# Splitting 36 of 48 key, query and value weights ahead of time and keeping their parts in DRAM

## The chip, the cores and the metric

The kernel runs on one core of a Trainium2 chip. The metric is the device time of one execution in microseconds (us), the median of three runs. TensorE is called PE, VectorE DVE, ScalarE ACT, GpSimd POOL and SyncE SP; PEld is PE's loading of the stationary operand. SP computes nothing here, it issues DMAs.

## The reference

Two residual blocks act on one sequence of 512 tokens with 1024 channels, all in float32. The first block has a sliding window attention layer and a pooling layer. The second has two layers of a mixer and a feed forward each:

```python
for l in range(DEPTH):                       # DEPTH = 2
    h = rmsnorm_2(x, attn_norm[l])
    proj = h @ w_in[l]                       # keys, queries and values of both kinds of heads
    sb_q, sb_k, sb_v, df_q, df_k, df_v = split(proj)
    sb_out = stick_breaking_attention(sb_q, sb_k, sb_v)        # 8 heads of 64
    df_out = differential_attention(rope(df_q), rope(df_k), df_v, lam)   # 4 pairs
    x = x + concat(sb_out, norm(df_out)) @ w_o[l]
    h = rmsnorm_2(x, mlp_norm[l])
    x = x + relu(h @ w_ff1[l])**2 @ w_ff2[l]                   # 1024 -> 4096 -> 1024
```

A stick-breaking head needs a running product over the keys of each row of scores, and so a scan.

## The kernel before

The activations lie transposed, 8 tiles of 128 channels by 512 tokens. Each product with a weight keeps float32 accuracy with three passes in a rounded format: a weight `w` is split into a high part `whi` (ACT copies it in the rounded format, L385) and a low part `wlo` (DVE subtracts, L388), the activations likewise into `xh` and `xl`, and PE adds whi·xh, whi·xl and wlo·xh in PSUM. One weight tile is 128 by 8 by 128, 512 KB; `lin` runs its 24 matmuls of 512 columns. For values, `lin_tokens` takes two such tiles (two halves) and runs 96 matmuls of 256 columns.

`weights` is the helper all of them call: it has `fetch` load the tile into `wst` (2 buffers) by a DMA on SP, then makes `whi` and `wlo` (3 buffers each). So ACT can split a weight as soon as PE has finished the weight three before it. A program names the order of PE's work: `lin` yields between its 8 steps, and the heads of the mixer (`sb_head` for stick-breaking, `df_head` for differential attention) are tasks which PE's order weaves between those steps. In a stick-breaking head each query tile goes through scores on PE, a mask on DVE (L1056), a sigmoid on ACT (L1058), 1 - w on ACT (L1061, tile `sbl`), a scan on DVE (L1064, `sbr`), a product on DVE (L1065, `sbw`), and then back to PE, which transposes it (`flip`, L358); ACT and DVE split the transposed tile into `wth` and `wtl` (L1078, L1079).

The whole program is built twice. After the first build `Plan` prices every instruction (`cost`), simulates the engines, and gives an order for PE, ACT, DVE, POOL and SP; the second build is bound to those orders. Every engine takes its instructions strictly in order, so an instruction that waits holds all behind it, and on SP a DMA that waits holds the later DMAs.

The stages on the time axis of the profile: sliding window attention until about 200 us, the pooling layer (`pool_layer`) until about 360, the first mixer until 600, the first feed forward (`ff_layer`) until 960, the second mixer until 1200, the second feed forward until the end. In a mixer 24 weight tiles are needed before the output projection: 8 of keys, 8 of queries, 8 halves of values.

Of the kernel before, what the change touches and what calls it, by code (L numbers as in the profile page):

```python
# [105 lines left out]
class Plan:  # L106
# [91 lines left out]
    def cost(self, k, i):  # L198
        def free(x):
            return math.prod(n for _, n in list(x.ap)[1:])  # L200

        def psum(x):
            return "PSUM" in str(type(x.bass_ap.tensor)).upper()

        aps = [x for x in i.outs if type(x).__name__ == "PhysicalAccessPattern"]
        src = [x for x in i.ins if type(x).__name__ == "PhysicalAccessPattern"]
        e, op = self.eng[k], str(i.opcode)
        n = max([free(x) for x in aps if x.memref] or [0])
        if op == "DMACopy":
            self.dur[k] = 1040.0 if e == "Pool" else 60.0  # L210
            self.bytes[k] = 4.0 * min(math.prod(m for _, m in x.ap) for x in aps + src)
        elif e == "PE":
            self.dur[k] = max(107.0, (n + 32) / 2.4)
        elif e == "Activation":
            one = sum(1 for x in src[1:] if free(x) == 1) + (len(aps) > 1)
            self.dur[k] = 1300.0 if not aps else n / 1.2 + (51.0 if psum(src[0]) else 93.0) + 93.0 * one
        elif e == "DVE":
            small = sum(1 for x in src[1:] if free(x) == 1) + (len(aps) > 1)
            fast = op in ("TensorCopy", "TensorScalarPtr") and len(src) - small <= 1 and not any(map(psum, src + aps))
            self.dur[k] = n / (1.92 if fast else 0.96) + 69.0 + (61.0 if small else 0.0)  # L220
            self.port[k] = fast or sum(1 for x in src if free(x) > 1 and not psum(x)) > 1
        else:
            self.dur[k] = 147.0 + 2.105 * n
            self.port[k] = op != "Memset"
# [83 lines left out]
def two_blocks_kernel(ctx: ExitStack, tc: tile.TileContext, a, out, log, orders=()):  # L308
# [13 lines left out]
    def open_pool(name, tags, side=None):  # L322
        pool = tc.alloc_tile_pool(name=name, bufs=1, side=side, reuse_waits="tile")
        log["pools"].append((name, True))
        where.update({t: pool for t in tags.split()})
        return pool
# [39 lines left out]
    def fetch(src, nk=KT, first=None):  # L366
# [5 lines left out]
            order(d, acts.pop("xdma"))  # L372
        return st

    def weights(src, nk=KT):
        with tc.high_priority():
            st = staged.pop(0) if staged else fetch(src, nk)
            hi = sb([P, KT, P], F32R, "whi", 3)
            lo = sb([P, KT, P], F32R, "wlo", 3)
            if early:  # L380
                early.pop()
                nc.vector.tensor_copy(hi[:, :nk, :], st[:, :nk, :])  # L382
                nc.vector.tensor_sub(lo[:, :nk, :], st[:, :nk, :], f32(hi[:, :nk, :]))  # L383
            else:
                c = nc.scalar.activation(hi[:, :nk, :], st[:, :nk, :], AF.Copy)  # L385
                if "x" in acts:
                    order(c, acts.pop("x"))
                low[0].tensor_sub(lo[:, :nk, :], st[:, :nk, :], f32(hi[:, :nk, :]))  # L388
        return hi, lo
# [17 lines left out]
    def lin(src, xs, tag="lin"):  # L407

        nk = len(xs)
        hi, lo = weights(src, nk)  # L410
        if spread[0]:
            spread[0] += 1
            tag = ("lin", "sc")[spread[0] % 2]
        ps = yield from take_bank(tag)
        for k in range(nk):
            if isinstance(xs[k], Val):
                if xs[k].t is None or xs[k].t > pe.clock:
                    yield xs[k]
                xh, xl = xs[k].v
            else:  # L420
                xh, xl = xs[k]
            mm(ps, hi[:, k, :], xh, k == 0, False)
            mm(ps, hi[:, k, :], xl, False, False)
            mm(ps, lo[:, k, :], xh, False, k == nk - 1)
            yield None
        return ps
# [365 lines left out]
    def add_to_x(k, ps):  # L792
        nc.vector.tensor_add(x[k], x[k], ps)  # L793
        drained(ps)
# [163 lines left out]

    def pool_layer(nrm, nxt):
        pin = a["pool_in"]  # L960
        pool = open_pool("pool", "u ws pz pe pth ptl tnh og uh ul")
        outs = [Val() for _ in range(8)]
        ps_ = [Val() for _ in range(8)]
        As = [Val() for _ in range(8)]

        def on_u(t, ps):
            w = POOL_WINDOWS[t // 2]

            def go(r):
                u = sb([P, 16 + S], F32, "u", 2)  # L970
                nc.gpsimd.memset(u[:, 0:16], 0.0)
                nc.vector.tensor_mul(u[:, 16:], ps, r)
                drained(ps)
                s, sh, c = u, 1, 0
                while sh < w:
                    n = sb([P, 16 + S], F32, "ws", 3)
                    c += sh
                    nc.gpsimd.tensor_add(n[:, c:], s[:, c:], s[:, c - sh:16 + S - sh])
                    s = n
                    sh *= 2  # L980
                pz = sb([P, S], F32, "pz", 2)
                nc.vector.scalar_tensor_tensor(pz, s[:, 16:], 1.0 / w, u[:, 16:],
                                               op0=ALU.mult, op1=ALU.subtract)
                e = sb([P, 16], F32, "pe", 2)
                nc.vector.tensor_mul(e, s[:, 16:32], inv[:, t // 2, :])
                nc.vector.tensor_sub(pz[:, 0:16], e, u[:, 16:32])
                put(ps_[t], split(pz, "pth", "ptl", 4, [P, S]), 8000.0)

            after(nrm.r, go)

        def on_z(t, ps):
            after(nrm.r, lambda r: put(As[t], silu2(evac(ps, r)), 1500.0))

        def on_mix(f, ps):
            def go(_):
                og = sb([P, S], F32, "og", 2)
                nc.vector.scalar_tensor_tensor(og, ps, hscale[:, f:f + 1], As[f].v,
                                               op0=ALU.mult, op1=ALU.mult)
                drained(ps)
                put(outs[f], split(og, "uh", "ul", 8, [P, S]), 2000.0)  # L1000
            after(As[f], go)

        mixw = None
        spread[0] = 1
        for g in range(4):
            for t in (2 * g, 2 * g + 1):
                ps = yield from lin(pin[t], nrm.xs)
                on_u(t, ps)
            for t in (2 * g, 2 * g + 1):
                ps = yield from lin(pin[8 + t], nrm.xs)  # L1010
                on_z(t, ps)
            if g % 2 == 0:
                mixw = weights(a["mix"][g // 2])
            for d in range(2):
                for k in range(2):
                    yield ps_[2 * g + k]
                ps = yield from take_bank("sc")
                for k in range(2):
                    c = (g % 2) * 4 + d * 2 + k
                    th, tl = ps_[2 * g + k].v  # L1020
                    mm(ps, mixw[0][:, c, :], th, k == 0, False)
                    mm(ps, mixw[0][:, c, :], tl, False, False)
                    mm(ps, mixw[1][:, c, :], th, False, k == 1)
                yield None
                on_mix(2 * g + d, ps)
        for k in range(KT):
            ps = yield from lin(a["pool_out"][k], outs)
            add_to_x(k, ps)
            nxt(k)
        spread[0] = 0  # L1030
        close_pool(pool)
# [143 lines left out]
        put(val, split(o, "dh", "dl", 4, [P, S]), 6000.0)  # L1175

    def mixer_layer(l, nrm, old, x_done, xd, nxt):
        w2 = a["w_in2"][l]
        low[0] = nc.vector
        mix = open_pool(f"mix{l}", "uh ul cs mdf qs pkh pkl v")  # L1180
        inner = []
# [61 lines left out]
            pe.spawn(task())  # L1243

        for i in range(8):
            c = (4, 0) if i < 4 else (12, 8)
            if i >= 2:
                yield heads[i - 2]
            ps = yield from lin(w2[c[0] + i], nrm.xs, "sc" if i == 1 else "lin")
            on_k(i, ps)  # L1250
            ps = yield from lin(w2[c[1] + i], nrm.xs, "sc" if i == 1 else "lin")
            on_q(i, ps)
            if i % 2 == 0:
                ps = yield from lin_tokens(a["v2"][l][i // 2], nrm.xs, "pv" if i == 0 else "lin")
                on_v(nrm, ps, Vs[2 * i:2 * i + 4] if i < 4 else Vs[4 + i:6 + i])
            pe.spawn(sb_pair(i) if i < 4 else df_pair(i))
        low[0] = nc.vector
# [24 lines left out]


    def ff_layer(l, nrm, nxt, end=None):
        ff = open_pool(f"ff{l}", "uh ul ev2")

        def on_1(u, ps):
            def go(r):
# [12 lines left out]
        def ff1(c, j, U):  # L1301
            ps = yield from lin(a["w_ff1"][l][8 * c + j], nrm.xs)
            U.append(Val())
            on_1(U[-1], ps)

        spread[0] = 1
        U = []
# [278 lines left out]
```

## Time and profile before

| | us |
|---|---|
| median of three runs | 1567.04 (1566.33 to 1567.07) |
| the profiled execution | 1568.69 |
| its span from the first to the last instruction | 1566.8 |
| PE busy | 1531.6 |
| DVE busy | 1114.5 |
| ACT busy | 778.4 |
| POOL busy | 117.6 |

A busy time is the union of an engine's instructions in the span. Matmuls are pipelined: in the record a matmul of 512 columns lasts some 390 ns, though the next one starts well before it ends. Stretches of the span are named by their start and end in us. The DMAs moved 147.21 MB, a mean of 94 GB/s.

### The profile page before, as it was taken

The numbers are of one execution on the slowest core, as the hardware profiler recorded it, in microseconds if no ns is written. First come the engines' busy times: TensorE is split into PE (matmuls) and PEld (weight loads), VectorE is DVE, ScalarE is ACT, GpSimd is POOL, SyncE is SP. The second block draws the span as 40 slices with busy tenths as digits, with TensorE's granted clock in tenths as the row PEclk, the third lists the DMA queues.
The fourth block names the chain that finished last, engine by engine and source line by source line (L and its number), as shares of the span: only waits on it lengthen the run. The fifth ranks groups of instructions, "written<-read, shape, count | busy, mean of one in ns | idle before, by whom it ended". The sixth has DMA issues, their size and how long they took to land.

```text
span 1566.8 us, 20047 instructions
## 1 busy us (share of the span) xinstructions
PE 1531.6 (98%) x7478; PEld 1276.1 (81%) x7478; DVE 1114.5 (71%) x1929; ACT 778.4 (50%) x1387; POOL 117.6 (8%) x125
## 2 busy tenths in 40 slices
PE   9999999999999999999999999999999999999997
PEld 7878888888778878888888888778888888888886
DVE  7899886778999988536354555899998635445454
ACT  6677563356788866222122234778876312222233
POOL 0000002400000000101010101000000201011010
PEclk9999999999999999999999999999999999999998
DMA  5211332334112223222332234212133323323221
GB/s 178 81 63 47 118 125 94 115 101 142 54 55 65 77 82 128 95 94 94 106 95 96 95 128 135 68 49 73 38 104 115 108 94 95 102 95 100 94 94 68
DMA packets 48227, 147.21 MB, mean 94 GB/s; under 512 B 5488, under 2 KB 7680, under 8 KB 48128
## 3 DMA queue, kind: packets, MB, share of 16 engines
q1 hardware_dynamic: 43824, 136.73, 26.6%
q0 software_dynamic: 1632, 5.22, 1.0%
q10 hardware_dynamic: 2672, 3.97, 0.8%
q8 instruction: 59, 0.97, 0.2%
q14 instruction: 40, 0.33, 0.1%
HBM read 139.60 MB, written 6.29 MB: 93 GB/s over the span
## 4 chain that ended last, share of the span: by engine, by line
PE 76%; DVE 15%; ACT 6%; issue 2%; DMA 1%; DVEq 0%; ACTq 0%; POOLq 0%
PE lin L351 43%; PE sc L351 28%; PE pv L351 4%; DVE sbr L1064 3%; DVE sbw L1065 1%; DVE wlo L388 1%; DVE wtl L1079 1%; DVE qs L713 1%; ACT sqt L1105 1%; PE tr L358 1%; ACT whi L385 1%; ACT p L827 1%; DVE ev L701 1%; DVE pkl L746 1%; DVE sc L1056 0%
## 5 line engine op out<-in xcount | busy, mean ns | idle before, releaser
L385 ACT ACTIVATE whi<-wst 128x1024 fp32r<-128x1024 f32 (+1 forms) x268 | 263.0, 983 | 588.7 <-PE lin L351 274.8
L388 DVE TENSOR_TENSOR wlo<-wst,whi 128x1024 fp32r<-128x1024 f32 (+1 forms) x268 | 354.7, 1324 | 42.6 <-ACT whi L385 41.6
L351 PE MATMUL lin<-xh,whi 128*128 128x512 f32 x672 | 266.7, 397 | 1.6 <-DVE whi L382 1.6
L351 PE MATMUL lin<-xh,wlo 128*128 128x512 f32 x672 | 264.3, 393 | 0.5 <-DVE wlo L383 0.5
L351 PE MATMUL lin<-xl,whi 128*128 128x512 f32 x672 | 264.5, 394 | 0.0
L351 PE MATMUL lin<-uh,whi 128*128 128x512 f32 (+1 forms) x480 | 187.7, 391 | 1.5 <-DVE xh L1263 1.5
L351 PE MATMUL lin<-uh,wlo 128*128 128x512 f32 (+1 forms) x480 | 186.8, 389 | 0.0
L351 PE MATMUL lin<-ul,whi 128*128 128x512 f32 (+1 forms) x480 | 185.6, 387 | 0.0
L351 PEld LDWEIGHTS lin<-xh,wlo 128*128 128x128 f32 x672 | 126.5, 188 | 26.3 <-DVE wlo L383 0.9
L351 PEld LDWEIGHTS lin<-xh,whi 128*128 128x128 f32 x672 | 126.5, 188 | 25.5 <-issue 2.3
L351 PEld LDWEIGHTS lin<-xl,whi 128*128 128x128 f32 x672 | 126.6, 188 | 23.9 <-DVE xl L636 0.5
L351 PE MATMUL sc<-xh,whi 128*128 128x512 f32 x368 | 143.9, 391 | 0.1
L351 PE MATMUL sc<-xh,wlo 128*128 128x512 f32 x368 | 143.7, 391 | 0.0
L351 PE MATMUL sc<-xl,whi 128*128 128x512 f32 x368 | 143.3, 389 | 0.0
L1295 POOL TENSOR_TENSOR ev<-ev 128x512 f32<-128x512 f32 x64 | 68.6, 1071 | 658.9 <-DVE ev L1290 658.9
L793 DVE TENSOR_TENSOR xm<-xm,lin 128x512 f32<-128x512 f32 x38 | 26.2, 688 | 115.2 <-PE lin L351 115.2
L351 PEld LDWEIGHTS lin<-uh,wlo 128*128 128x128 f32 x480 | 90.2, 188 | 19.5
L351 PEld LDWEIGHTS lin<-uh,whi 128*128 128x128 f32 x480 | 90.3, 188 | 19.3 <-DVE xh L1263 2.0
L351 PEld LDWEIGHTS lin<-ul,whi 128*128 128x128 f32 x480 | 90.2, 188 | 18.6
L351 PE MATMUL sc<-uh,whi 128*128 128x512 f32 (+1 forms) x232 | 90.3, 389 | 0.0
L351 PE MATMUL sc<-uh,wlo 128*128 128x512 f32 (+1 forms) x232 | 90.0, 388 | 0.0
L351 PE MATMUL sc<-ul,whi 128*128 128x512 f32 (+1 forms) x232 | 89.2, 385 | 0.0
(250 smaller groups left out, 2818.7 us busy)
## 6 DMA issues: line engine op xcount, KB each, us to landing
wst<-in_w_ff_dram SPq DMA_DIRECT2D x128, 512.0 KB, 3.5
wst<-in_w_in_dram SPq DMA_DIRECT2D x32, 512.0 KB, 3.5
wst<-in_attn_in_dram SPq DMA_DIRECT2D x18, 512.0 KB, 3.6
wst<-in_pool_in_dram SPq DMA_DIRECT2D x16, 512.0 KB, 3.5
wst<-in_v_dram SPq DMA_DIRECT2D x16, 512.0 KB, 3.5
wst<-in_w_o_dram SPq DMA_DIRECT2D x32, 256.0 KB, 2.6
wst<-in_attn_out_dram SPq DMA_DIRECT2D x16, 256.0 KB, 2.7
wst<-in_pool_out_dram SPq DMA_DIRECT2D x8, 512.0 KB, 3.5
```

Of the source, the lines that this page charges most:

```text
L351: i = nc.tensor.matmul(o, lhsT=l, rhs=r, start=start, stop=stop, skip_group_check=True)
L358: nc.tensor.transpose(o, i, ident)
L385: c = nc.scalar.activation(hi[:, :nk, :], st[:, :nk, :], AF.Copy)
L388: low[0].tensor_sub(lo[:, :nk, :], st[:, :nk, :], f32(hi[:, :nk, :]))
L701: nc.vector.tensor_mul(t, ps, r)
L713: nc.vector.tensor_sub(t[o0:o0 + 64, :], src[p0:p0 + 64, :], f32(t[p0:p0 + 64, :]))
L746: nc.vector.tensor_sub(lo[p0:p0 + 64, :], s, f32(h[p0:p0 + 64, :]))
L793: nc.vector.tensor_add(x[k], x[k], ps)
L827: nc.scalar.activation(pt[:, j, :w], pt[:, j, :w], AF.Exp, scale=-1.0, bias=negm[:, j:j + 1], accum_out=den[:, j:j + 1])
L1064: nc.vector.tensor_tensor_scan(r[:, 1:n][:, ::-1], back, back, 1.0, op0=ALU.mult, op1=ALU.min)
L1065: nc.vector.tensor_mul(w[:, :n - 1], w[:, :n - 1], r[:, 1:n])
L1295: nc.gpsimd.tensor_mul(t2, t, t)
```

## The change

The weights of keys, queries and values of a mixer get names (`mixer_weights`). `split_ahead` loads one into a new tile `ast`, splits it into `ahi` on ACT and `alo` on DVE, and writes both to DRAM tiles `wd`, all three DMAs on SP; `ast`, `ahi` and `alo` have 2 buffers each. The pooling layer does so for 12 of the 24 weights of the first mixer (every second one in the order of use), the first feed forward for all 24 of the second mixer, one call beside one weight of the layer's own. Where a weight has been kept, `weights` loads `whi` and `wlo` from DRAM with two DMAs on SP in place of the load of `wst`, the copy on ACT and the subtraction on DVE. Besides, the planner's price of a scan on DVE goes from n/0.96 to n/0.48 ns, plus 69 ns as before.

```diff
-            self.dur[k] = n / (1.92 if fast else 0.96) + 69.0 + (61.0 if small else 0.0)
+            scan = "Scan" in type(i).__name__ + op or getattr(i, "is_tensor_tensor_scan", False)
+            self.dur[k] = n / (1.92 if fast else 0.48 if scan else 0.96) + 69.0 + (61.0 if small else 0.0)
...
+    def split_ahead(name, src):
+
+        st = sb([P, KT, P], F32, "ast", 2)
+        nc.sync.dma_start(st, src)
+        hi = sb([P, KT, P], F32R, "ahi", 2)
+        nc.scalar.activation(hi, st, AF.Copy)
+        lo = sb([P, KT, P], F32R, "alo", 2)
+        nc.vector.tensor_sub(lo, st, f32(hi))
+        kept = []
+        for t in (hi, lo):
+            ctr[0] += 1
+            d = dpool.tile([P, KT, P], F32, tag=f"wd{ctr[0]}", name=f"wd{ctr[0]}")
+            nc.sync.dma_start(d, f32(t))
+            kept.append(d)
+        ahead[name] = kept
...
     def weights(src, nk=KT):
+        if isinstance(src, list):
+            with tc.high_priority():
+                parts = [sb([P, KT, P], F32R, tag, 3) for tag in ("whi", "wlo")]
+                for t, d in zip(parts, src):
+                    nc.sync.dma_start(f32(t), d)
+            return parts
...
     def pool_layer(nrm, nxt):
...
+        todo = list(mixer_weights(0).items())[1::2][:12]
...
                 ps = yield from lin(pin[t], nrm.xs)
                 on_u(t, ps)
+                if todo:
+                    split_ahead(*todo.pop(0))
...
             ps = yield from lin(a["pool_out"][k], outs)
+            if todo:
+                split_ahead(*todo.pop(0))
...
-            ps = yield from lin(w2[c[0] + i], nrm.xs, "sc" if i == 1 else "lin")
+            ps = yield from lin(weight(w2, ("k", l, i)), nrm.xs, "sc" if i == 1 else "lin")
...
     def ff_layer(l, nrm, nxt, end=None):
-        ff = open_pool(f"ff{l}", "uh ul ev2")
+        ff = open_pool(f"ff{l}", "uh ul ev2 ast ahi alo")
+        todo = list(mixer_weights(l + 1).items()) if l + 1 < DEPTH else []
...
             on_1(U[-1], ps)
+            if todo:
+                split_ahead(*todo.pop(0))
```

SP in the first feed forward, before: one load of a weight follows another.

```order
L368 DMA wst_6749<-in_w_ff_dram 128x1024
L368 DMA wst_6781<-in_w_ff_dram 128x1024
L368 DMA wst_6813<-in_w_ff_dram 128x1024
L368 DMA wst_6845<-in_w_ff_dram 128x1024
L368 DMA wst_6877<-in_w_ff_dram 128x1024
```

The same place on SP now; `ast` is the load of a weight of the second mixer, `wd` the DRAM copy of a part.

```order
L369 DMA wst_6999<-in_w_ff_dram 128x1024
L369 DMA wst_7031<-in_w_ff_dram 128x1024
L402 DMA wd_6931<-ahi_6927 128x1024
L393 DMA ast_7279<-in_w_in_dram 128x1024
L402 DMA wd_6933<-alo_6929 128x1024
L402 DMA wd_7236<-ahi_7232 128x1024
L393 DMA ast_7328<-in_w_in_dram 128x1024
L402 DMA wd_7238<-alo_7234 128x1024
L369 DMA wst_7063<-in_w_ff_dram 128x1024
L369 DMA wst_7095<-in_w_ff_dram 128x1024
```

Between two pairs of loads stand the six DMAs of two splits, and that pattern goes on until the 24 splits are done.

DVE in the second mixer, while the first stick-breaking heads run, before: `wlo` of a half of values stands among the steps of the heads.

```order
L1079 TENSOR_TENSOR wtl_9036<-sc_9157,wth_9035 128x2x128
L1056 TENSOR_TENSOR sc_9146<-sc_9146,msb 128x128
L1065 TENSOR_TENSOR sbw_9125<-sbw_9125,sbr_9129 128x511
L701 TENSOR_TENSOR ev_9327<-lin_9271,rstd_8796 128x512
L388 TENSOR_TENSOR wlo_9446<-wst_9443,whi_9445 128x1024
L1064 SCALAR_TENSOR_TENSOR sbr_9154<-sbl_9152 128x383
L1079 TENSOR_TENSOR wtl_9012<-sc_9162,wth_9011 128x3x128
L1065 TENSOR_TENSOR sbw_9150<-sbw_9150,sbr_9154 128x383
```

The same steps on DVE now (`sbr` is the scan, which is printed as a scalar-tensor-tensor):

```order
L1124 TENSOR_TENSOR wtl_9362<-sc_9481,wth_9361 128x2x128
L1101 TENSOR_TENSOR sc_9470<-sc_9470,msb 128x128
L1110 TENSOR_TENSOR sbw_9449<-sbw_9449,sbr_9453 128x511
L741 TENSOR_TENSOR ev_9649<-lin_9593,rstd_9130 128x512
L1109 SCALAR_TENSOR_TENSOR sbr_9478<-sbl_9476 128x383
L753 TENSOR_TENSOR qs_9651<-ev_9649,qs_9651 64x512
L1101 TENSOR_TENSOR sc_9492<-sc_9492,msb 128x128
L1124 TENSOR_TENSOR wtl_9338<-sc_9486,wth_9337 128x3x128
```

The subtraction of the weight is gone from between the product and the next scan; the heads' steps keep their sequence but for a step or two.

SP in the second mixer now, where before each weight had one load of `wst`:

```order
L414 DMA whi_9306<-wd_6735 128x1024
L414 DMA wlo_9307<-wd_6737 128x1024
L414 DMA wlo_9375<-wd_6786 128x1024
L414 DMA whi_9374<-wd_6784 128x1024
L414 DMA wlo_9590<-wd_6835 128x1024
L414 DMA whi_9589<-wd_6833 128x1024
```

Two DMAs for each weight, which go straight into the buffers that PE reads, so that SP waits there for PE.

## Rows read from the trace of the kernel before

**Rows 1.** The page: PE's busy line; PE and DVE in 40 slices.

```profile
PE 1531.6 (98%) x7478; PEld 1276.1 (81%) x7478; DVE 1114.5 (71%) x1929; ACT 778.4 (50%) x1387; POOL 117.6 (8%) x125
...
PE   9999999999999999999999999999999999999997
...
DVE  7899886778999988536354555899998635445454
```

**Rows 2.** Busy time by stretch; last columns PE clock, DMA share, GB/s.

```profile
1000.00:1120.00 120.00, 111.79 (x658) 94.85 (x657) 112.43 (x233) 97.33 (x194) 0.00 (x0) 1.00 0.18 58
400.00:520.00 120.00, 112.23 (x658) 94.75 (x657) 112.49 (x232) 97.64 (x195) 0.00 (x0) 1.00 0.18 58
...
1120.00:1200.00 80.00, 78.83 (x413) 66.67 (x412) 74.46 (x171) 59.86 (x125) 2.19 (x4) 1.00 0.27 87
200.00:320.00 120.00, 120.00 (x531) 99.27 (x529) 90.95 (x129) 50.93 (x68) 31.24 (x32) 1.00 0.34 110
640.00:780.00 140.00, 140.00 (x615) 115.26 (x614) 64.58 (x64) 33.39 (x37) 11.48 (x11) 1.00 0.30 98
```

**Rows 3.** Timeline of ACT, first feed forward: start, us, instruction, idle before.

```profile
702.12 1.06 ACT L385 ACTIVATE whi<-wst 128x1024 fp32r<-128x1024 f32 x1 [4.43 <-PE sc L351]
...
707.61 1.06 ACT L385 ACTIVATE whi<-wst 128x1024 fp32r<-128x1024 f32 x1 [3.85 <-PE lin L351]
...
713.05 1.06 ACT L385 ACTIVATE whi<-wst 128x1024 fp32r<-128x1024 f32 x1 [3.86 <-PE sc L351]
```

**Rows 4.** Timeline of DVE in the same stretch.

```profile
703.21 2.09 DVE L388 TENSOR_TENSOR wlo<-wst,whi 128x1024 fp32r<-128x1024 f32 x1 [0.18 <-ACT whi L385]
```

**Rows 5.** Busy time by stretch, where PE runs values alone, 256 columns each.

```profile
966.00:976.00 10.00, 10.00 (x86) 10.00 (x85) 5.93 (x7) 4.29 (x6) 0.26 (x1) 1.00 0.29 95
```

**Rows 6.** PE's instructions by line, 1000 to 1120: count, busy us, mean ns.

```profile
L351 PE MATMUL lin<-xh,whi 128*128 128x512 f32 x69 | 27.9, 405 | 0.0
...
L351 PE MATMUL lin<-wlo,xh 128*128 128x256 f32 x71 | 20.6, 290 | 0.0
...
L358 PE MATMUL sc<-sq,sbw 128*128 128x128 f32 x71 | 12.9, 278 | 4.9 <-DVE sbw L1065 4.2 <-ACT sbw L1058 0.7
L351 PE MATMUL sc<-qs,pkh 128*128 128x128 f32 (+3 forms) x39 | 12.8, 335 | 0.7 <-ACT sbw L1058 0.5 <-DVE wtl L1079 0.2
...
L351 PE MATMUL pv<-wth,v 128*128 128x512 f32 (+3 forms) x32 | 10.1, 326 | 0.9 <-ACT wth L1078 0.9
```

**Rows 7.** Busy time of L388 (the subtraction) alone, by stretch.

```profile
400.00:520.00 120.00, 15.83 (x13) 1.00 0.18 58
1000.00:1120.00 120.00, 15.70 (x13) 1.00 0.18 58
```

**Rows 8.** Chain of work that ended last by line, 400:520, then 1000:1120.

```profile
by line: DVE sbr L1064 14.2%; DVE sbw L1065 7.6%; DVE wtl L1079 7.4%; issue 6.5%; ACT sqt L1105 5.9%; PE lin L351 5.2%; DVE qs L713 5.2%; DVE wlo L388 5.0%; ACT whi L385 3.4%; ACT dp L1131 3.1%; DVE pkl L746 2.9%; DVE o L1096 2.7%; DVE ev L
...
by line: PE lin L351 15.9%; DVE sbr L1064 13.4%; DVE sbw L1065 7.0%; DVE wtl L1079 6.6%; ACT sqt L1105 5.9%; DVE qs L713 4.0%; issue 4.0%; DVE wlo L388 4.0%; PE pv L351 3.5%; ACT whi L385 3.4%; ACT dp L1131 2.9%; DVE sc L1056 2.5%; DVE ev L
```

**Rows 9.** Waits of PE, 980 to 1200: us, times, longest.

```profile
PE sc L358 <- DVE sbw L1065: 4.2, 7, 1.1
```

**Rows 10.** DVE by form, 980 to 1120: count, busy us, mean ns.

```profile
L1064 DVE TENSOR_TENSOR_SCAN sbr<-sbl 128x511 f32<-128x511 f32 x8 | 9.7, 1217 | 0.1
```

**Rows 11.** DMA issues: count, KB each, us from issue to landing.

```profile
wst<-in_w_in_dram SPq DMA_DIRECT2D x32, 512.0 KB, 3.5
...
wst<-in_w_o_dram SPq DMA_DIRECT2D x32, 256.0 KB, 2.6
...
xd<-x_in SPq DMA_DIRECT2D x8, 256.0 KB, 2.3
```

**Rows 12.** Stretches with full DMA queues: at the start, and eight writes to DRAM.

```profile
2.00:14.00 12.00, 9.84 (x24) 6.18 (x23) 7.28 (x13) 5.66 (x9) 2.10 (x4) 0.87 0.99 357
375.00:380.00 5.00, 5.00 (x33) 4.51 (x32) 5.00 (x8) 2.35 (x2) 0.00 (x0) 1.00 0.98 363
```

More of the change, by code (lines that the diff above doesn't have):

```diff
@@ L373, in fetch, with mixer_weights, weight @@
         return st
-    def weights(src, nk=KT):
+    ahead = {}
+    def mixer_weights(l):
+        w = {}
+        for i in range(8):
+            c = (4, 0) if i < 4 else (12, 8)
+            w["k", l, i] = a["w_in2"][l][c[0] + i]
+            w["q", l, i] = a["w_in2"][l][c[1] + i]
+            if i % 2 == 0:
+                for s in range(2):
+                    w["v", l, i // 2, s] = a["v2"][l][i // 2][s]
+        return w
+    def split_ahead(name, src):
[12 more added lines that the diff above has]
+        ahead[name] = kept
+    def weight(w, name):
+        return ahead.get(name, w[name])
+    def weights(src, nk=KT):
+        if isinstance(src, list):
[4 more added lines that the diff above has]
+            return parts
         with tc.high_priority():
@@ L960, in pool_layer @@
         pin = a["pool_in"]
-        pool = open_pool("pool", "u ws pz pe pth ptl tnh og uh ul")
+        pool = open_pool("pool", "u ws pz pe pth ptl tnh og uh ul ast ahi alo")
+        todo = list(mixer_weights(0).items())[1::2][:12]
         outs = [Val() for _ in range(8)]
@@ L1177, in mixer_layer @@
     def mixer_layer(l, nrm, old, x_done, xd, nxt):
-        w2 = a["w_in2"][l]
+        w2 = mixer_weights(l)
         low[0] = nc.vector
@@ L1245, in mixer_layer @@
         for i in range(8):
-            c = (4, 0) if i < 4 else (12, 8)
             if i >= 2:
                 yield heads[i - 2]
-            ps = yield from lin(w2[c[0] + i], nrm.xs, "sc" if i == 1 else "lin")
+            ps = yield from lin(weight(w2, ("k", l, i)), nrm.xs, "sc" if i == 1 else "lin")
             on_k(i, ps)
-            ps = yield from lin(w2[c[1] + i], nrm.xs, "sc" if i == 1 else "lin")
+            ps = yield from lin(weight(w2, ("q", l, i)), nrm.xs, "sc" if i == 1 else "lin")
             on_q(i, ps)
             if i % 2 == 0:
-                ps = yield from lin_tokens(a["v2"][l][i // 2], nrm.xs, "pv" if i == 0 else "lin")
+                ps = yield from lin_tokens([weight(w2, ("v", l, i // 2, s)) for s in range(2)], nrm.xs, "pv" if i == 0 else "lin")
                 on_v(nrm, ps, Vs[2 * i:2 * i + 4] if i < 4 else Vs[4 + i:6 + i])
```

## The prediction, made before the changed kernel ran

> **What bounds the kernel now.** I read the page first. PE is busy 98% of the span and shows a 9 in all slices but the last, while DVE comes to 9 only in the window attention and in the two mixers [rows 1]. That busy share hides waits, because a matmul of 512 columns lasts some 400 ns in the record and its end covers a gap behind it. So I count at PE's pace instead. In the feed forward, where nothing makes PE wait, ACT takes up a new weight every 5.47 us (702.12, 707.61, 713.05), which are 24 matmuls, 0.228 us each [rows 3]. Where values run alone 84 whole matmuls of 256 columns go through in 10 us, 0.12 us each [rows 5]. By a straight line through the two, 128 columns cost about 0.07 us and a mix with a mean of 320 about 0.147; these two are estimates.
>
> The stretch of the second mixer in which the stick-breaking heads run, 1000 to 1120, then needs of PE: three groups of 69 at 0.228 (47.2 us), three of 71 values at 0.12 (25.6), 71 flips and 11 like them at 0.07 (5.7), scores and products of the heads, 39 and 32, twice each, at 0.147 (20.9), and some 2 us for 14 others [rows 6]. That is 101.4 of 120 us: PE loses about 18.6 us there, though the busy column shows only 8.2 us idle [rows 2]. DVE is busy for 112.4 us, 94%, and the first mixer has the same numbers within 0.5 us [rows 2]. PE's largest wait in the second mixer is the flip, for the product on DVE that follows the scan [rows 9]. So in both stretches PE has time to give back and DVE sets the pace. In the pooling layer and in the feed forward PE is busy without a gap [rows 2]: there nothing can be won, only lost.
>
> [...]
>
> **What the change takes from DVE and ACT.** In 1000 to 1120 there are 13 subtractions, 15.7 us of DVE, and all go. In 400 to 520 there are also 13, 15.8 us [rows 7]; every second weight is kept, so 7 go, 8.5 us. DVE would then need 96.7 us in the second mixer and 104.0 in the first; ACT, with 97 us in either [rows 2], loses its copies with them.
>
> What the stretch shrinks to has two estimates. By load: no engine is filled better than DVE is today, 94%. The second mixer is then held by PE, 101.4 / 0.94 = 107.9 us, a gain of 12.1; the first by DVE, 104.0 / 0.94 = 110.6, a gain of 9.4. By the chain of work that ended last: the subtraction and the copy together hold 7.4% of 120 us in the second mixer (8.9 us) and 8.4% in the first (10.1 us, of which 7 of 13 go, 5.4) [rows 8]. A chain re-forms along other work, so this is no floor, but the order of the heads' own steps is nearly kept, so the load alone is too kind. I take the middle: 10.5 and 7.4 us. In 1120 to 1200, with the differential heads, DVE is busy 74.5 of 80 us [rows 2], and two kept weights fall there in the second mixer and one in the first: between nothing and 1.2 us for each of the three; I take 1.5 in all. Together **19.4 us**. The upper end is the whole 18.6 of the second mixer, 13 of the first (its DVE load at 97%) and 3, so 34; the lower end is the subtractions' share of the chain without the copies, 4.0% and 5.0% x 7/13 of 120 us [rows 8], 8 us.
>
> **The planner's price.** A scan over 511 columns took 1217 ns [rows 10]; by the code it was priced at 601 ns and is now at 1133. Nothing executes differently by that, only the order can move. PE's and DVE's orders in the heads move by a step or two. I take 0, with 3 us either way.
>
> **What it adds in the pooling layer.** 12 copies on ACT, 12 subtractions on DVE and 36 DMAs on SP. POOL works there, and beside POOL's work a subtraction took 2.09 us in the feed forward [rows 4], against 1.21 in the mixers (15.7 / 13) [rows 7]. So DVE gets 15 to 25 us more; it has 29 us free in 200 to 320 alone [rows 2] and the layer goes on to 360. ACT is idle for more than half. A subtraction that stands ahead of an urgent one holds it for 2 us at most, and the weights are split well ahead of use (below). I take 1 us, range 0 to 4.
>
> **What it adds in the first feed forward.** 24 splits. DVE is busy for 64.6 of 140 us, ACT for 33.4 [rows 2], so both have room. What is tight is SP and the DMA queues. A pair of weights takes PE 10.94 us, and in the steady pattern 8 DMAs of 524 KB go with it, 4.19 MB. With full queues the DMAs moved 357 GB/s at the start and 363 while eight tiles were written to DRAM [rows 12]: 4.19 MB take 11.5 to 11.7 us. So each of the 12 pairs falls behind by 0.7 us, 8 us in all. The slack: a weight's subtraction is done at 705.3 [rows 4], while the buffer freed at 702.1 is read two weights later, at 713.0, 7.7 us; and its successor is loaded from 705.3 on and lands 3.5 us later [rows 11], at 708.8, where ACT takes it at 713.05 [rows 3], 4.2 us. That is 11.9 us before PE waits, more than the 8. Reading and writing at once is not in the trace. The nearest rows are the full queues; the other end is the share of the feed forward itself, 98 GB/s at a share of 0.30 [rows 2], so 327 GB/s at a share of one: 12.8 us a pair, 22 us behind, 10 us lost. Below zero there is nothing, since PE has no gap to fill. I take 1 us, range 0 to 10. On SP every weight load now queues behind writes that wait for ACT and DVE; these are done long before, as the load of a split is issued a pair earlier.
>
> [...]
>
> **What it adds in the mixers.** A kept weight costs two DMAs on SP that wait for PE to free the buffers. From there the first lands in 3.5 us [rows 11], the second 1.4 us later at 363 GB/s, 4.9 us; PE needs it two weights later, 10.9 us, and more where heads are woven in. Before, copy and subtraction took about 2.3 us of the same time. Hidden, cost 0; DMA share there is 0.18 [rows 2]. If that cover were gone, each of 36 weights would cost what it is late.
>
> **The sum.** 19.4 - 1 - 1 = 17.4 us. The profiled execution took 1568.7 us, 1.9 above its span, so 1551.3; it lies 1.7 above the median of the runs, so I predict **1550 us** against 1567.0.
>
> **The rivals.**
>
> *The heads' latency stays* (1561 us). The order of PE is nearly the old one, and a flip waits for a sequence of mask, sigmoid, scan and product; if that sequence and not the load of DVE makes PE wait, only the subtractions on the chain go, 8 us less 2. For it: PE waits for that product above all [rows 9]. Against it: DVE is 94% busy, so most of the sequence is queueing.
>
> *Nearly all the waits go* (1534). 34 us less 1, if the heads get ahead of PE once DVE is free. Against it: no stretch of the mixers has both engines that full.
>
> *The feed forward starves* (slower). SP takes DMAs in order; if the 8 of a pair take longer than PE's 10.94 us by more than the slack spread over 12 pairs, every weight comes late. The gain is eaten when 12 x (P - 10.94) - 11.9 passes 18.4, that is at P = 13.5 us or 310 GB/s. At 280 GB/s it loses 37 us: 1586. For it: 310 is not far below the 327 above, and the queues were never full with both directions. Against it: both rows with full queues, one of loads and one of writes, are near 360.
>
> *Weights come late in the mixers* (1567 or above). If each of 36 waits 0.5 us on its landing, 18 us come back. The landing would have to take twice its 4.9 us.
>
> *The change moves the order and no more* (1567): the shuffled orders cost what the splits give. The printed order shows the subtractions gone, which speaks against it.
>
> **How the numbers follow.** Forecast (1543 to 1557) 0.48; latency stays 0.18; nearly all goes 0.10; starving 0.12, of which a third stays below the old time; late weights 0.07; order only 0.05. A measurement of this kernel tells 0.2%, 3.1 us, from no change. Faster by more: 0.48 + 0.16 + 0.10 + 0.03 = 0.77; within 0.2%: 0.09; slower 0.14. The range reaches from the upper end of the gain, 1534, to 1566, just above the rival with the least gain.
>
> **What would show it.** In the changed profile, DVE in the stick-breaking stretch of the second mixer falls from 112 to about 97 us and the stretch to near 109; the first mixer's to near 112. PE stays without a gap in the pooling layer and the first feed forward, where the DMAs come to a share over 0.9. PE waits nowhere on `whi` or `wlo`. I am wrong if the feed forward grows by more than 3 us, if PE waits for DMAs of kept parts, or if DVE's load falls and PE's waits stay.

## The result, and the profile after

The changed kernel takes 1553.28 us (median of four, 1553.13 to 1554.08) beside 1566.68 for the kernel before on the same chip: a ratio of 0.9917 [0.9905, 0.9928], 13.4 us faster. Predicted were 1550 (1534 to 1566). The profiled execution took 1553.20 us and has a span of 1551.3, 1.9 less than its time, as before. In what follows two executions are left out as slow ones, one of e12_margin (2163.57 us) and one of before beside the first experiments (3929.31).

The page of after answers to [rows 1]: span, busy time of each engine, and the 40 slices of DVE, the DMA engines and their rate.

```profile
span 1551.3 us, 20346 instructions
PE 1527.2 (98%) x7478; PEld 1273.8 (82%) x7478; DVE 1101.8 (71%) x1929; ACT 779.5 (50%) x1387; POOL 127.0 (8%) x125
DVE  8899898878998989656354554888898635455455
...
DMA  5221379535223227999322236333233332322222
GB/s 194 69 68 49 115 271 343 207 119 181 82 82 116 96 70 275 395 353 363 110 95 96 95 118 216 134 136 127 99 104 119 99 105 94 98 95 95 95 95 68
```

PE and DVE have as many instructions as before. In the slices of the two mixers (the 11th to the 16th and the 26th to the 31st) DVE still shows an 8 or a 9, and in the first feed forward the DMA engines now show a 9 at up to 395 GB/s.

The stretches of [rows 2] in after (busy time with the count of instructions; last columns PE clock, DMA share, GB/s):

```profile
1000.00:1120.00 120.00, 117.29 (x724) 102.30 (x723) 103.19 (x237) 92.19 (x197) 0.00 (x0) 1.00 0.33 122
1120.00:1200.00 80.00, 78.97 (x366) 64.31 (x365) 71.16 (x152) 55.88 (x110) 3.22 (x5) 1.00 0.34 106
200.00:320.00 120.00, 120.00 (x531) 99.26 (x530) 101.51 (x140) 62.73 (x80) 33.42 (x32) 1.00 0.75 269
640.00:780.00 140.00, 140.00 (x615) 115.13 (x614) 73.17 (x78) 48.58 (x52) 15.23 (x10) 1.00 0.77 284
```

In 1000 to 1120 PE runs 724 matmuls where it ran 658. In the pooling layer and in the feed forward PE has no gap, as before, with the same 531 and 615 matmuls, though DVE has 10.6 and 8.6 us more to do there. (The stretch from 1000 no longer covers quite the same work, since after is some 8 us ahead by then.)

To see where the time went I number PE's matmuls (7478 in every trace) from 0 in the order of their starts and take the time between two numbers near the stages' edges: 988 to 1701 holds the pooling layer, 1701 to 3017 the first mixer, 3017 to 4579 the first feed forward, 4579 to 5894 the second mixer, 5894 to the last one the second feed forward. Each entry is the difference of two starts in one trace, in us:

| kernel | pooling layer | first mixer | first feed forward | second mixer | second feed forward |
|---|---|---|---|---|---|
| before | 161.85 | 243.17 | 356.89 | 242.96 | 350.93 |
| after | 161.86 | 236.86 | 357.26 | 236.49 | 350.94 |
| difference | 0 | -6.3 | +0.4 | -6.5 | 0 |

The stages add up to 12.4 us, and the tail behind the last matmul's start gives 0.5 more. The medians differ by 13.4, the two spans by 15.5. That excess arises in the first 30 us, where the kernels do the same: matmul 100 starts at 30.03 in before, and between 27.5 and 29.4 in after and the experiments (27.53 in after). Stretch 8 to 16 in before, same columns:

```profile
8.00:16.00 8.00, 6.88 (x20) 4.53 (x21) 7.54 (x11) 5.93 (x10) 0.00 (x0) 0.79 0.95 362
```

and in after:

```profile
8.00:16.00 8.00, 7.60 (x30) 5.42 (x31) 7.81 (x13) 7.10 (x13) 0.00 (x0) 1.00 0.87 330
```

In that execution of before the data came later (PE's matmul 20 starts at 12.6 us beside 10.5 in after), and PE had a granted clock of 0.79 there. I take that for a mishap of one execution and no effect of the change: the median of before lies 2.0 us under this execution.

### The profile page after: what moved, and what is told of

The parts are those of the page before. It is cut to its first block, busy times and chain, and to the rows that moved or that the text cites. A ratio compares the mean times of both kernels' runs of the same rounds, so it can differ in the third digit from the quotient of the medians.

```text
span 1551.3 us, 20346 instructions
## 1 busy us (share of the span) xinstructions
PE 1527.2 (98%) x7478; PEld 1273.8 (82%) x7478; DVE 1101.8 (71%) x1929; ACT 779.5 (50%) x1387; POOL 127.0 (8%) x125
## 4 chain that ended last, share of the span: by engine, by line
PE 80%; ACT 9%; DVE 9%; issue 2%; DMA 1%; ACTq 0%; DVEq 0%; POOLq 0%
PE lin L352 45%; PE sc L352 29%; PE pv L352 4%; ACT sqt L1150 2%; PE sc L359 1%; DVE sbr L1109 1%; PE tr L359 1%; ACT dp L1176 1%; ACT p L867 1%; DVE wlo L428 1%; ACT sbl L1106 1%; ACT pkh L785 1%; ACT pkh L784 1%; DVE ev L741 1%; ACT sbw L1103 0%
## 5 line engine op out<-in xcount | busy, mean ns | idle before, releaser
L425 ACT ACTIVATE whi<-wst 128x1024 fp32r<-128x1024 f32 (+1 forms) x232 | 224.3, 970 | 478.3 <-PE lin L352 205.2
L428 DVE TENSOR_TENSOR wlo<-wst,whi 128x1024 fp32r<-128x1024 f32 (+1 forms) x232 | 299.8, 1294 | 29.9 <-ACT whi L425 29.2
L1340 POOL TENSOR_TENSOR ev<-ev 128x512 f32<-128x512 f32 x64 | 75.9, 1186 | 652.3 <-DVE ev L1335 652.3
L352 PEld LDWEIGHTS lin<-uh,wlo 128*128 128x128 f32 x480 | 90.1, 188 | 19.5
```

Of the source, the lines that this page charges most:

```text
L352: i = nc.tensor.matmul(o, lhsT=l, rhs=r, start=start, stop=stop, skip_group_check=True)
L1340: nc.gpsimd.tensor_mul(t2, t, t)
```

## The experiments

Two theories stood against each other. *The load*: the mixers run at DVE's pace, so each subtraction taken from DVE (and copy from ACT) shortens them, and the scan's new price hardly matters. *The price*: the engines keep to orders made from prices; with the scan at half its price PE's order asks for a product before it can be there, and no relief of DVE helps until that is put right. The stages of the experiments, in us as in the table above:

| kernel | first mixer | first feed forward | second mixer |
|---|---|---|---|
| e1_price | 240.61 | 356.93 | 240.79 |
| e2_splits | 242.61 | 357.25 | 242.70 |
| e3_pool | 236.85 | 357.09 | 240.24 |
| e4_ff | 240.62 | 357.15 | 237.42 |
| e5_ffhalf | 240.37 | 356.81 | 236.79 |
| e6_dve_only | 236.65 | 357.36 | 237.34 |
| e7_act_only | 237.37 | 356.80 | 239.81 |
| e8_twice | 236.98 | 417.65 | 236.40 |
| e9_noscan | 235.63 | 356.91 | 235.29 |
| e10_over | 242.64 | 356.67 | 235.03 |
| e11_half | 236.87 | 357.11 | 236.83 |
| e12_margin | 235.82 | 356.09 | 236.33 |

### The price alone, and the splits alone

The kernel before with nothing but the new price:

```diff
-            self.dur[k] = n / (1.92 if fast else 0.96) + 69.0 + (61.0 if small else 0.0)
+            scan = "Scan" in type(i).__name__ + op or getattr(i, "is_tensor_tensor_scan", False)
+            self.dur[k] = n / (1.92 if fast else 0.48 if scan else 0.96) + 69.0 + (61.0 if small else 0.0)
```

> The kernel before with the planner's new price of a scan alone, no weight split ahead. Theory (the gain is DVE's load in the mixers): the price moves the order a little and no work, so no change within 0.2%, 1564 to 1570 us, and the stick-breaking stretch of each mixer keeps its DVE load of 94%. Rival (the gain is the better order): 1554 to 1560 us.

The changed kernel with the old price (the same lines the other way round):

> The changed kernel with the old price of a scan, so the splits alone. Theory (load of DVE): as the changed kernel, 1553 us within 3. Rival (the better order): most of the gain goes, 1560 us or more.

Measured: the price alone 1562.25 us, 0.997 [0.9959, 0.9981], 4.3 faster; the splits alone 1565.83, 0.9996 [0.9986, 1.0005], no change. Together they give 13.4. The two confidence intervals don't meet, and that of the splits alone contains no change. In stages: the price takes 2.6 and 2.2 us from the two mixers, the splits alone 0.6 and 0.3, both 6.3 and 6.5.

The same stretch of 160 us in the second mixer (PE, PEld, DVE, ACT, POOL busy with their counts, clock, DMA share, GB/s), in before:

```profile
985.00:1145.00 160.00, 151.79 (x888) 129.60 (x887) 151.26 (x322) 131.78 (x268) 1.66 (x3) 1.00 0.19 61
```

in e1_price:

```profile
985.00:1145.00 160.00, 154.53 (x898) 131.33 (x897) 152.30 (x330) 135.13 (x274) 2.19 (x4) 1.00 0.22 70
```

in e2_splits:

```profile
985.00:1145.00 160.00, 153.62 (x890) 129.62 (x889) 133.75 (x311) 117.20 (x250) 2.19 (x4) 1.00 0.34 117
```

and in after:

```profile
985.00:1145.00 160.00, 156.17 (x920) 134.28 (x919) 139.96 (x323) 123.25 (x264) 2.19 (x4) 1.00 0.35 123
```

The row of e2_splits is the case against the load: DVE falls from 151.3 to 133.8 us, 84%, ACT to 117.2, and yet PE runs 890 matmuls, two more than before. Here engines with room to spare do not make PE go faster. With the true price the same splits let it run 920. (The four kernels are not equally far at 985 us, so the counts compare roughly. Over the same matmuls, 4733 to 5619, they take 159.8, 156.4, 159.5 and 153.2 us in the order of the rows, with DVE busy for 151.1, 148.6, 133.2 and 133.6: e2_splits and after differ by 0.4 us in DVE's busy time and by 6.3 us in time.)

What PE waits for is read from the view of the product `sbw`: idle time of the engine ahead of the instructions of this tile, until the product was there (us, times), whole run. All of these are PE's matmuls, but for three of PEld (2.6 us) in e2_splits. In before:

```profile
  DVE sbw L1065: 7.0, 12
```

in e1_price:

```profile
  DVE sbw L1066: 0.4, 1
```

in e2_splits:

```profile
  DVE sbw L1109: 7.9, 12
```

and in after:

```profile
  DVE sbw L1110: 1.3, 3
```

These go with the price and not with the load: 12 waits remain when DVE is relieved under the old price, one remains when DVE is as full as ever under the new. They are not the whole account. All waits of PE over 0.15 us come to 8.7 and 9.3 us in the two mixers of before, 5.6 and 5.6 in e1_price, 8.1 and 6.8 in e2_splits, 3.8 and 4.1 in after; so the second mixer of e2_splits has 2.5 us less of them than before and is only 0.3 us shorter, which these views don't explain.

The programs' orders suggest why. For each of the 64 query tiles I counted the matmuls that stand in PE's order between the last one of its scores and the first flip of its product. That lead is what covers the mask, sigmoid, scan and product:

| kernel | mean lead, matmuls | smallest |
|---|---|---|
| before | 38.4 | 23 |
| e1_price | 41.6 | 24 |
| e2_splits | 34.7 | 19 |
| after | 39.7 | 23 |

Under the old price the planner spends DVE's freed time on bringing flips forward, from 38.4 to 34.7 matmuls, counting on a scan of 601 ns where it takes 1217 [rows 10]. The product isn't ready, and PE stands. Under the true price the lead grows, and shrinks with the splits only to 39.7. (Matched in the traces by the order of starts alone, the means come out at 38.6, 42.8, 34.9 and 39.9: the same picture, good to about one matmul.) In the trace of before, from 127 to 511 columns the scan's mean grows from 415 to 1217 ns and the product's from 282 to 683, which is 2.09 ns a column beside 1.04.

### Each place of the splits

No splits in the first feed forward; then, apart from that, none in the pooling layer:

```diff
-        todo = list(mixer_weights(l + 1).items()) if l + 1 < DEPTH else []
+        todo = []
```

> The changed kernel with the 12 splits of the pooling layer alone, the second mixer as before. Theory: the first mixer is shorter by 6.5 us as in the changed kernel, the pooling layer costs nothing, 1560 us. If the pooling layer's splits cost what they give: 1564 us or more.

```diff
-        todo = list(mixer_weights(0).items())[1::2][:12]
+        todo = []
```

> The changed kernel with the 24 splits of the first feed forward alone, the first mixer as before. Theory: the second mixer is shorter by 6.5 us, the feed forward costs nothing though its DMA share is near 1.0 while the splits run: 1560 us. If the two parts need each other, the sum of the gains of this run and of the one with the pooling layer alone differs from 13.4 us by more than 2.

Measured: 1557.93 us, 0.9945 [0.9928, 0.9961], with the pooling layer's twelve alone, and 1557.64, 0.9944 [0.9929, 0.9959], with the feed forward's 24 alone. Against e1_price each gives 4.3 to 4.6 us, in its own mixer: the mixer without kept weights takes 240.2 or 240.6 us, like both in e1_price, the other 236.9 or 237.4. With 4.3 for the price the sum is 4.3 + 4.3 + 4.6 = 13.2, against 13.4 measured. So, once the price is right, the places add up, and twelve weights bring as much as 24. These four runs also speak against mere luck of the orders: a mixer with kept weights takes 236.5 to 237.4 us and one without 240.2 to 240.8, whichever of the two mixers it is.

### Fewer weights

Twelve of the 24 in the first feed forward, without and with the pooling layer's twelve:

```diff
-        todo = list(mixer_weights(l + 1).items()) if l + 1 < DEPTH else []
+        todo = list(mixer_weights(l + 1).items())[1::2] if l + 1 < DEPTH else []
```

> New price; of the splits only every second weight of the second mixer, 12 in the first feed forward, none in the pooling layer. The first mixer gained as much by 12 kept weights as the second by 24. If the relief saturates once DVE is no longer full: as with all 24, 1557.6 us within 1. If the gain goes with the number of weights: about 1560 us.

> The changed kernel with every second weight of the second mixer split ahead, 12 in the first feed forward in place of 24, beside the 12 of the pooling layer. If the relief saturates: the same time as the changed kernel, 1553.3 us within 1, and the feed forward's stretch of full DMA queues is half as long. If the second half of the weights still gives something: 1555 to 1558 us.

Measured: 1557.49 us, 0.994 [0.9925, 0.9955], beside 1557.64 with 24; and 1554.16, 0.9919 [0.9906, 0.9933], beside 1553.28. The second mixer takes 236.8 in both, against 237.4 and 236.5 with all 24. The second twelve bring at most some 0.9 us: relief beyond half of the weights finds next to nothing left to shorten.

### One engine's part alone

The kept low part is loaded, while the high part is copied from the raw weight as before (DVE relieved alone); then the kept high part is loaded and DVE subtracts (ACT relieved alone). Both make the same splits ahead as after.

```diff
-        return ahead.get(name, w[name])
+        return ahead[name] + [w[name]] if name in ahead else w[name]
...
-                for t, d in zip(parts, src):
-                    nc.sync.dma_start(f32(t), d)
+                st = fetch(src[2])
+                nc.scalar.activation(parts[0], st, AF.Copy)
+                nc.sync.dma_start(f32(parts[1]), src[1])
```

> The changed kernel, but a kept weight's low part alone comes from DRAM; its raw tile is loaded too and ACT copies the high part as before. So DVE is relieved and ACT is not. If the gain beyond the price is DVE's load: 1553 to 1555 us. If it is ACT's copies: 1560 to 1563 us, near the price alone.

```diff
...
-                for t, d in zip(parts, src):
-                    nc.sync.dma_start(f32(t), d)
+                st = fetch(src[2])
+                nc.sync.dma_start(f32(parts[0]), src[0])
+                nc.vector.tensor_sub(parts[1], st, f32(parts[0]))
```

> The changed kernel, but a kept weight's high part alone comes from DRAM; its raw tile is loaded too and DVE subtracts as before. So ACT is relieved and DVE is not. If the gain beyond the price is DVE's load: 1560 to 1563 us, near the price alone. If it is ACT's copies: 1553 to 1555 us.

Measured: DVE alone 1553.98 us, 0.9919 [0.9904, 0.9934]; ACT alone 1557.03, 0.9936 [0.9921, 0.9951]. From the 1562.25 of the price alone that is 8.3 and 5.2 us, where both give 9.0. They overlap, so neither is "the" relieved engine. DVE's part is nearly enough by itself. That ACT's alone brings more than half, in the first mixer 3.2 of 3.7 us, though DVE's load there hardly falls, I cannot explain by a load; it may be the copy's place in the sequence from load to PE, or just another order. It stays open.

### Relief without splits

The kernel before, with the running product left out: the scan is replaced by a plain product of the same shape, which the old price fits far better: 601 ns for 511 columns, where a product of that length takes 683 in before and the scan 1217.

```diff
-            nc.vector.tensor_tensor_scan(r[:, 1:n][:, ::-1], back, back, 1.0, op0=ALU.mult, op1=ALU.min)
+            nc.vector.tensor_mul(r[:, 1:n][:, ::-1], back, back)
```

> The kernel before with the scan replaced by a product of the same operands' sizes (the running product over the keys is left out), which the old price, 601 ns for 511 columns, fits. DVE is relieved of some 11 us in each mixer, less than by the 24 splits, and the order is made from true prices. Theory (the order made from a wrong price eats the relief): 1553 to 1558 us. Rival (relief of DVE gives little whatever the price, as the splits alone did): 1563 us or more.

Measured: 1552.08 us, 0.9905 [0.9889, 0.9922], 14.8 faster, 7.5 and 7.7 us in the two mixers. Here the price is nearly true, because the instruction was changed to fit it, and PE's order is the old one, matmul for matmul, lead 38.4 and all. About as much comes out as with the whole change, without one DMA more. It shows that the old order is a good one when DVE is as fast as its price. It doesn't part load from latency, since the plain product is both less work and sooner done.

### Too high a price

```diff
-            self.dur[k] = n / (1.92 if fast else 0.48 if scan else 0.96) + 69.0 + (61.0 if small else 0.0)
+            self.dur[k] = n / (1.92 if fast else 0.32 if scan else 0.96) + 69.0 + (61.0 if small else 0.0)
```

> The changed kernel with a scan priced at n/0.32 + 69 ns, 1666 ns for 511 columns where it takes 1217 in the trace. Theory (orders must be made from true prices, since each engine keeps to them): the heads are put too late, part of the gain goes, 1555 to 1560 us. Rival (only an underpriced scan harms, by flips that come too early on PE): no change, 1553 us within 1.

Measured: 1558.51 us, 0.9946 [0.993, 0.9963], 5.2 slower than after. The stages keep me from reading it as the cost of a wrong price: the second mixer is 1.5 us faster than in after, the first 5.8 slower. The longest of PE's waits in the first mixer of e10_over (us, times, longest):

```profile
PE lin L352 <- DVE v L807: 3.1, 1, 3.1
```

and the stretch right behind it, busy times, clock, DMA share and rate:

```profile
478.00:490.00 12.00, 11.16 (x50) 9.43 (x51) 9.66 (x25) 6.72 (x15) 0.00 (x0) 0.86 0.25 87
```

The first matmul of a weight stood 3.1 us for values that DVE had still to take out of a PSUM tile, and the mean granted clock was 0.86 behind that. Inside this stretch it stood at 0.50:

```profile
479.50:482.70 3.20, 3.20 (x13) 2.90 (x13) 3.05 (x6) 1.89 (x3) 0.00 (x0) 0.50 0.04 10
```

In before, where the granted clock was 0.50 from 10.8 to 14.2 us, matmuls of 512 columns start 0.43 us apart, beside 0.227 at 1.00. By that about half of these 3.2 us are lost, an estimate of 1.6 us, so that this one wait and the clock behind it make up 4.7 of the 5.8 us. A price that is too high made one mixer better and one worse. So orders scatter by some us per mixer, and of the two wrong prices only the low one is shown to do harm in both. Each kernel here is one order, so a part of any single difference can be such scatter.

### The starving rival

Each part is written to DRAM twice, so 12 DMAs go with a pair of weights where after has 8.

```diff
+        for t in (hi, lo):
+            ctr[0] += 1
+            d = dpool.tile([P, KT, P], F32, tag=f"wd{ctr[0]}", name=f"wd{ctr[0]}")
+            nc.sync.dma_start(d, f32(t))
         ahead[name] = kept
```

> The changed kernel, where each part of a split is written to DRAM a second time, to a place that nobody reads: five DMAs for a split in place of three. If the DMA queues were near their limit for PE (8 DMAs of 524 KB in 10.9 us at a share of 1.0), 12 DMAs for a pair of weights take 17 us, and the feed forward loses up to 60 us. If the order spreads the splits over more weights, as there are 64 in the layer and 24 splits: no change within 2 us of the changed kernel, 1553 to 1555 us, with the share near 1.0 for longer.

Measured: 1642.88 us, 1.0477 [1.046, 1.0494], 89.6 slower than after: 60.4 us in the first feed forward, 28 in the pooling layer, nothing in the mixers. Two stretches of its feed forward, columns as above:

```profile
640.00:680.00 40.00, 34.26 (x136) 26.79 (x135) 19.76 (x23) 14.16 (x16) 9.09 (x6) 0.91 1.03 412
680.00:720.00 40.00, 31.28 (x120) 23.42 (x119) 17.47 (x18) 11.10 (x11) 1.04 (x1) 0.91 1.02 399
```

and what waited for the weights there, 600 to 900 (us, times, longest):

```profile
ACT whi L429 <- DMA wst<-in_w_ff_dram: 41.6, 17, 9.9
...
PE sc L352 <- ACT whi L429: 24.3, 10, 4.4
...
PE sc L352 <- DVE wlo L432: 14.5, 11, 1.9
```

The chain of the rival *the feed forward starves* stands there link by link: full queues, ACT late for the load, PE late for both parts, 120 to 136 matmuls in 40 us instead of 177. The queues moved some 405 GB/s, and it was too little: 12 DMAs of 524 KB are 6.29 MB, 15.5 us where PE has 10.94. The prediction's rule, 12 x (15.5 - 10.94) - 11.9, gives 43 us lost; 60 were. Without the slack of 11.9 it gives 55, so nothing of that slack shows here; but the rule also leaves out the granted clock, 0.91 in both stretches, and the two can't be told apart. The planner does reckon with the queue (`DMA_RATE`, 360 bytes a ns, in its simulation), and its order kept the loads so late all the same; why is open. In after the DMAs of 600 to 720 (packets and rate, the queue's share, then issues with count, KB and us to landing) read:

```profile
DMA packets 12186, 44.47 MB, mean 371 GB/s; under 512 B 1344, under 2 KB 1344, under 8 KB 12180
...
q1 hardware_dynamic: 12180, 44.39, 98.1%
...
wd<-ahi SPq DMA_DIRECT2D x22, 512.0 KB, 6.9
wst<-in_w_ff_dram SPq DMA_DIRECT2D x22, 512.0 KB, 6.7
```

ACT's waits in after, 600 to 760:

```profile
ACT whi L425 <- DMA wst<-in_w_ff_dram: 20.1, 13, 4.1
ACT whi L425 <- PE sc L352: 13.0, 5, 4.4
```

and ACT's waits in before, 600 to 760:

```profile
ACT whi L385 <- PE sc L351: 53.1, 13, 4.4
ACT whi L385 <- PE lin L351: 50.7, 13, 4.4
ACT whi L385 <- DMA wst<-in_w_ff_dram: 4.2, 3, 2.2
```

The cover has become thin in after: ACT used to wait for PE to free a buffer (103.8 us against 4.2 for a load) and now waits for the load more (20.1 against 13.0 in the row shown and 4.4 behind `lin`), only not yet so long that PE feels it. e11_half, which keeps the gain to within 0.9 us with half the splits there, would by that be the safer kernel, which no run here tests.

### A margin at PE

The planner adds a fixed time between an instruction on ACT or DVE and the one on PE that waits for it. Here both are 150 ns longer:

```diff
-            ("Activation", "PE"): 271, ("PE", "DVE"): 196, ("Pool", "DVE"): 74, ("DVE", "PE"): 202,
+            ("Activation", "PE"): 421, ("PE", "DVE"): 196, ("Pool", "DVE"): 74, ("DVE", "PE"): 352,
```

> The changed kernel where the planner adds 150 ns to the delays from DVE to PE and from ACT to PE, so that in PE's order a step that waits for either comes a little later behind other matmuls. If the waits that PE has left come from steps placed too tightly, they shrink: 1548 to 1552 us. If the planner's delays are true as they are, as its other prices are, later is worse or the same: 1553 to 1557 us.

Measured: 1550.8 us (the median of four executions, 1550.28 to 1551.76), 0.9896 [0.9881, 0.9911], 2.5 faster than after and the fastest of all kernels here. The gain is scattered: 1.0 us in the first mixer, 1.2 in the feed forward, 0.6 ahead of the pooling layer, 0.2 in the second mixer (and its profiled execution began 1.6 later). Against the scatter of e10_over I take it for plausible that PE's order is too tight in general, not for shown.

## Why the prediction was right, and where it was not

The time came 3.3 us above the forecast and inside its own range. Part of that is luck, since two terms were off in opposite directions: the price, taken at 0 with 3 us either way, gives 4.3 us alone, and the splits, taken at 17.4 us, give 0.75 alone and 9.0 once the price is right. The steps fared unequally.

**PE has time to give back in the mixers, and the busy column hides most of it: right, with a smaller size.** Counted start to start, with a line through 0.227 and 0.12 us for 512 and 256 columns (as in rows 3 and 5) as the need of a matmul, PE lost 25.9 and 26.0 us in the two mixers of before and 19.6 and 19.5 in after. In excesses over 0.2 us after one matmul stand 12.6 and 12.6 of that in before, 5.7 and 6.4 in after; the smaller ones, 13 to 14 us a mixer, hardly changed. The floor of 101.4 us was too low: consecutive flips of 128 columns start 109 ns apart in the trace, not 70. For 82 of them that is 3.2 us, so some 15 us of the 18.6 could ever be won in that stretch.

**DVE sets the pace: this is the step that failed, with the planner's price as the term that was wrong.** I took the price at 0, since nothing executes differently by it, and put the whole gain on the load. The runs show that the load pays only behind the price: taken away under the old price it gives 0.75 us, which is no clear change, the price alone 4.3, the load under the true price 9 more. The sign I gave as one that would prove me wrong, "if DVE's load falls and PE's waits stay", is what e2_splits shows: DVE's load fell and the 12 waits for the product stayed. The printed order couldn't show it, because the harm lies not in which steps DVE does but in how soon PE's order asks for their result. The price was in the diff, and [rows 10] had the true duration beside it; 64 scans priced at half of their duration should have been followed into PE's order.

**The size of the gain: first mixer 6.3 where I had 7.4, second 6.5 where I had 10.5, and 1.5 for the differential heads on top that didn't appear apart.** The estimate by load said that twice the weights bring more. They don't (e5_ffhalf, e11_half): with half of the subtractions gone PE no longer waits for the product in the second mixer of either run, and what is left of its waits there, 3.9 us, is spread over nine waits for different steps of DVE and ACT. The rival *the heads' latency stays* was right so far: part of the waits were for a sequence that came too late, not for an engine that was full. Its price, 1561, was wrong, since the change repairs that sequence's place too.

The chain of work that ended last shows that it re-formed, 1000 to 1120 in after, beside [rows 8]:

```profile
by line: PE lin L352 33.7%; ACT sqt L1150 10.7%; PE pv L352 5.9%; PE sc L352 5.7%; PE sc L359 4.4%; ACT sbl L1106 3.1%; ACT qs L752 3.0%; issue 3.0%; ACT dp L1176 2.9%; ACT sbw L1103 2.6%; DVE sbr L1109 2.6%; ACT pkh L785 2.0%; DVE ev L741 
```

The scan has gone from 13.4% of it to 2.6% and PE's products with weights from 15.9% to 33.7%; `whi` and `wlo` are not in it.

**The pooling layer, 1 us: 0. The first feed forward, 1 us: 0.4 and no gap of PE there.** The working was right in kind, and e8_twice shows that the loss at its far end was no phantom. With 371 GB/s over 120 us, waits included, a pair's 4.19 MB take 11.3 us where I had 11.5 to 11.7. Against PE's 10.94 that is 0.4 us a pair and 4 us over twelve. PE never stood for a weight there, so the slack covered that much; that it reaches to 11.9 no run shows.

**Kept parts in the mixers, 0: right.** They land 3.3 and 4.1 us after their issue, in the median of 985 to 1145 in after:

```profile
whi<-wd SPq DMA_DIRECT2D x15, 512.0 KB, 3.3
wlo<-wd SPq DMA_DIRECT2D x15, 512.0 KB, 4.1
```

PE's waits hold neither `whi` nor `wlo` in 985 to 1185, and the mixers of e8_twice, e6_dve_only and after agree to 0.9 us.

**"The change moves the order and no more"** stood at 0.05. The order was not all, yet without the price the rest of the change gave no clear gain (e2_splits).

## What to carry to other kernels

Where engines run in orders made from prices, compare every instruction's measured duration with its price before you relieve any engine: here an underpriced step on the path turned relief into waits, and correcting the price costs nothing to try. Test load and order apart, by the same edit under both prices. When half of a relief brings the whole gain, take half, above all if the other half fills a queue that covers something else.

## What the runs showed of the chip that I had not expected

Reads and writes of DRAM together moved more than either row with full queues in before (357 and 363 GB/s, rows 12): 412 and 399 over 40 us each in the two stretches of e8_twice. Before comes to 398 over a shorter stretch, 10.8 to 14.2 us.

Writes to DRAM were hardly slower than loads, 6.9 us to landing beside 6.7 for the same size in the same full queues. And behind waits of PE the granted clock was lower in three places: the 3.1 us in e10_over were followed by the 3.2 us at 0.50 in the row shown, a wait of 1.6 us in before, which ends at 8.5 us, by 3.4 us at 0.50 from 10.8 on, and in the starved feed forward of e8_twice, with waits up to 4.4 us, the granted clock was 0.91 for the two stretches shown. In the mixers of before, with waits up to 1.1 us [rows 9], it stayed at 1.00 [rows 2]. That the wait is what lowers the clock, so that it costs more than its length, is my reading; no run varied the wait alone.
